# A two-layer attention trunk on one core: the softmax maximum is written already negated and scaled, and the step that scaled it goes

## The chip, the cores and the metric

The kernel runs on one core of a Trainium2 chip. The metric is device time in microseconds (us) of one execution, from three runs of each kernel. The engines are named as in the profile: PE (TensorE, with PEld for its weight loads), DVE (VectorE), ACT (ScalarE), POOL (GpSimd) and SP (SyncE, which here issues the DMAs). Each engine works through a fixed list of instructions in order and waits on semaphores that the other engines raise.

## What is computed

Two equal layers over 1024 tokens of width 1024. Each layer has two attention branches and a channel mixer; only the attentions' softmaxes matter here.

```python
# neighbourhood attention, 8 heads of 64: scores over an 8x16 window, scale = 64 ** -0.5 = 0.125
s = jnp.einsum('bhcd,ibhcjd->bhcij', q_r, k_nb).astype(jnp.float32) * scale
s = s + bias.transpose(0, 2, 1, 3)[None].astype(jnp.float32)
p = jax.nn.softmax(s.reshape(B, H, GRID_W, kh * kw), axis=-1)
...
# latent attention, 8 heads: q = rmsnorm(c_q, g_q) @ w_uq, scale = 96 ** -0.5
s = (jnp.einsum('bhqd,bkhd->bhqk', qn_b, k_nope)
     + jnp.einsum('bhqr,bkr->bhqk', qr_b, k_r))
p = jax.nn.softmax(s.astype(jnp.float32) * scale, axis=-1).astype(v.dtype)
```

`g_q` is a gain of 256 values per layer that multiplies the normalised latent before `w_uq` makes both parts of the query from it.

## The kernel before

One layer runs in stages, each of which keeps PE as the engine that all others feed: a token projection, the neighbourhood attention (NA) with the gate projections as filler between its units, the latent attention (MLA), a merge of both branches, an output projection, and the channel mixer. Everything is float32; products that need full precision are done as three matmuls of split operands (`mm3`, lines 208 to 210), so that a matmul of 512 columns is by far the commonest PE instruction.

**NA** (lines 595 to 641): 64 units a layer, each 128 queries by 384 keys. `unit_a` multiplies into the PSUM tile `sna` (L601), adds the bias table and takes the row maximum in one DVE instruction (L605), scales that maximum by -0.125 in a second, one column wide (L607), takes the exponential on ACT with the scaled maximum as its bias (L608), the reciprocal of the row sum on DVE (L609), and normalises on POOL (L610). `unit_b` transposes the result on PE (L618) and copies it to SBUF, half of the units on DVE (L621) and half on ACT (L623); `unit_c` multiplies by the values (L632).

**MLA** (lines 790 to 840): 64 units a layer, each 128 queries by 1024 keys. `unit_a` makes the scores in `smla`, a PSUM tile of two banks of which two are in rotation (six matmuls, L796), takes the maximum (L798), scales it by -96^-0.5 (L799), takes the exponential (L801), the reciprocal (L802), and normalises on POOL (L803). `unit_b` transposes (eight matmuls, L815) and copies the one half on ACT (L821), the other on DVE (L819); `unit_c` multiplies by the values (L830), 16 matmul instructions for every four units, which the trace records as 32. I call four units with their `unit_c` a block; there are 16 blocks a layer. Between the units stand the steps that prepare the next pair of heads (`prep_q` and `prep_k`, tiles `pqn` and `pkn`, with casts on ACT at L530 and subtractions on DVE at L531), and towards the end the loads and splits of the NA output for the merge (L852).

The order of an engine's list is not the order in which the code is written. The program is recorded unit by unit, and then a scheduler with its own estimate of every instruction's duration places each instruction on its engine where its inputs would be ready by that estimate. So a change of one DVE instruction can move matmuls. The exponential of unit n must have ended before the scores of unit n+2 are written, since two `smla` tiles rotate, and POOL must have normalised unit n before its transposes. These two are waits of PE.

Of the kernel before, what the change touches and what calls it, by code (L numbers as in the profile page):

```python
# [12 lines left out]
AF = mybir.ActivationFunctionType  # L13
ALU = mybir.AluOpType
AX = mybir.AxisListType
# [10 lines left out]
MLA_SCALE = 96 ** -0.5  # L26
# [11 lines left out]
def hybrid_trunk(  # L38
# [6 lines left out]
    V, A, G, T = nc.vector, nc.scalar, nc.gpsimd, nc.tensor  # L45
    depth = w_in.shape[0]
# [43 lines left out]
    def bank(s="pb"):  # L90
        return psb.tile([P, CH], F32, tag="pb", name=nm(s))
# [16 lines left out]
    col0 = {}  # L108
    cols = const.tile([P, 256], F32, name="cols")
# [11 lines left out]
    def turn_rows(t, n, base):  # L121
        ps = bank("pcols")
        tc.keep_in_program_order(T.transpose(ps[:, :n], t[:n, :], ident[:n, :n]))
        V.tensor_copy(cols[:, base:base + n], ps[:, :n])
# [55 lines left out]
    def ada_turn(l, j, acc):  # L180
        m = mods[l]
        for hh in range(2):
            ps = bank("pada")
            for k in range(4):
                T.transpose(ps[:, k * P:(k + 1) * P], acc[:, (4 * hh + k) * P:(4 * hh + k + 1) * P], ident)
            s = slice(8 * j + 4 * hh, 8 * j + 4 * hh + 4)
            V.tensor_reduce(m[:, s], ps[:].rearrange("p (a b) -> p a b", b=P), axis=AX.X, op=ALU.add)
        b0 = col0["b_ada"] + 48 * l + 8 * j
        V.tensor_tensor(m[:, 8 * j:8 * j + 8], m[:, 8 * j:8 * j + 8], cols[:, b0:b0 + 8], op=ALU.add)
        if j in (1, 4):  # L190
            t, g = (amix[l], "g_mix") if j == 1 else (amlp[l], "g_mlp")
            g0 = col0[g] + 8 * l
            V.tensor_scalar(t, m[:, 8 * j:8 * j + 8], 1.0, None, op0=ALU.add)
            V.tensor_tensor(t, t, cols[:, g0:g0 + 8], op=ALU.mult)
# [96 lines left out]
    ps = bank("ppos")  # L291
# [51 lines left out]
    for ch in range(2):  # L343
        for k in range(8):
            ps = bank("pyT")
# [10 lines left out]
    turn_rows(ta, na_, 0)  # L356
    turn_rows(tb, nb_, 128)

    ada_turn(0, 1, acc1)
    last = ada_sum(acc0, first_shift[5:], 5, pin)  # L360
    xT = [slab("xT") for _ in range(8)]
# [179 lines left out]
    def na_steps(l, h):  # L541

        tabs = {}
        for hd in range(2):
            for rg in range(2):
                t = pool["na"].tile([P, 12, 96], F32, name=nm(f"tab{hd}{rg}"))
                G.memset(t, NEG)
                tabs[hd, rg] = t

        def tables(pair, hd, rg):  # L550
            for r in range(8):
                row = 8 * rg + r
                st = min(max(row - 4, 0), 8)
                d0 = st - row + 7
                k0 = st - 4 * rg
                nc.sync.dma_start(tabs[hd, rg][r * 16:(r + 1) * 16, k0:k0 + 8, :], u_d[2 * pair + hd, :, d0:d0 + 8, :])

        st, vts = {}, {}

        def qk_weights(pair, n):  # L560
            st["w"] = whalves(kblock(w_in[l], (4 * n + pair) * P))

        def qk_unit(pair, n, ch):
            if ch == 0:
                st[pair, n] = [slab("st", dt=F32R) for _ in range(2)]
            ps = dense(st["w"], h[ch])
            for hd in range(2):
                dst = st[pair, n][hd][:, cs(ch)]
                if n == 0:
                    view = lambda t: t.rearrange("p (g r c) -> p r g c", g=4, c=16)  # L570
                    stacks(dst, ps[:].rearrange("p (r g c) -> p r g c", g=4, c=16), hd, view)
                else:
                    stacks(dst, ps, hd)

        def k_swap(pair):
            st[pair, 2] = [slab("st", dt=F32R) for _ in range(2)]
            for hd in range(2):
                swapped(st[pair, 2][hd], st[pair, 1][hd])

        def values(pair):  # L580
            vt = []
            for wi, w in enumerate(NA_WIN):
                if wi % 2 == 0:
                    vs = slab("vna", (P, 2, 4, P))
                for blk in range(4):
                    nc.sync.dma_start(
                        vs[:, wi % 2, blk, :],
                        v_d[:].rearrange("(b r c) d -> b r c d", r=4, c=64)[blk, :, w:w + 32, pair * P:(pair + 1) * P],
                    )
                vt.append(vs[:, wi % 2])  # L590
            vts[pair] = vt

        pts, po = {}, {}

        def unit_a(pair, rg, cg, hd):
            q1, k1, k2 = (st[pair, n][hd] for n in range(3))
            w = NA_WIN[cg]
            ps = pool["na_ps"].tile([P, 12, 32], F32, tag="S", name=nm("sna"))
            qs = q1[:, rg * CH + cg * P:rg * CH + (cg + 1) * P]
            for i, kk in enumerate((k1, k2)):  # L600
                T.matmul(ps, qs, kk[:].rearrange("p (r c) -> p r c", c=64)[:, 4 * rg:4 * rg + 12, w:w + 32],  # L601
                         start=i == 0, stop=i == 1)
            pt = pool["na"].tile([P, 12, 32], F32, tag="P", name=nm("pna"), bufs=4)
            sm = small()
            V.tensor_tensor_reduce(pt, ps, tabs[hd, rg][:, :, NA_KIND[cg] * 32:(NA_KIND[cg] + 1) * 32],  # L605
                                   op0=ALU.add, op1=ALU.max, scale=1.0, scalar=-3e38, accum_out=sm[:, 0:1])
            V.tensor_scalar(sm[:, 1:2], sm[:, 0:1], -0.125, None, op0=ALU.mult)  # L607
            A.activation(pt, pt, AF.Exp, bias=sm[:, 1:2], scale=0.125, accum_out=sm[:, 2:3])  # L608
            V.reciprocal(sm[:, 3:4], sm[:, 2:3])  # L609
            G.tensor_scalar(pt, pt, sm[:, 3:4], 1.0, op0=ALU.mult, op1=ALU.mult)  # L610
            pts[pair, rg, cg, hd] = pt

        def unit_b(pair, rg, cg, hd):
            pt = pts[pair, rg, cg, hd]
            pT = bank("pTna")
            pf = pt[:].rearrange("p a b -> p (a b)")
            for j in range(3):
                T.transpose(pT[:, j * P:(j + 1) * P], pf[:, j * P:(j + 1) * P], ident)  # L618
            t = pool["na"].tile([P, 384], F32, tag="pT", name=nm("ptna"), bufs=7)
            if (cg + hd) % 2:  # L620
                V.tensor_copy(t, pT[:, :384])  # L621
            else:
                A.copy(t, pT[:, :384])  # L623
            pts[pair, rg, cg, hd] = t

        def unit_c(pair, rg, cg):
            if cg == 0:
                po[pair, rg] = pool["na_ps"].tile([P, CH], F32, tag="po", name=nm("pona"))
            p = po[pair, rg]
            for j in range(3):  # L630
                for hd in range(2):
                    T.matmul(p[64 * hd:64 * hd + 64, cg * P:(cg + 1) * P],  # L632
                             vts[pair][cg][:, j + rg, 64 * hd:64 * hd + 64],
                             pts[pair, rg, cg, hd][:, j * P:(j + 1) * P], start=j == 0, stop=j == 2)
            if cg == 3:
                o = tmp("ona")
                V.tensor_copy(
                    o[:].rearrange("p (r g c) -> p r g c", g=4, c=16),
                    p[:].rearrange("p (g r c) -> p r g c", g=4, c=16),
                )  # L640
                nc.sync.dma_start(o_d[pair * P:(pair + 1) * P, cs(rg)], o)

        return qk_weights, qk_unit, k_swap, values, tables, unit_a, unit_b, unit_c


    def mla_steps(l):
# [143 lines left out]
        def unit_a(pair, q2, hd, qi):  # L790
            q1, k1, k2, qr = st[pair, hd]
            t = slice(q2 * 256 + qi * P, q2 * 256 + (qi + 1) * P)
            ps = pool["S"].tile([P, 1024], F32, tag="S", name=nm("smla"))
            for ch in range(2):
                for i, (a, b) in enumerate(((q1, k1), (q1, k2), (qr, d["Kr"]))):
                    T.matmul(ps[:, cs(ch)], a[:, t], b[:, cs(ch)], start=i == 0, stop=i == 2)  # L796
            sm = small()
            V.reduce_max(sm[:, 0:1], ps, axis=AX.X)  # L798
            V.tensor_scalar(sm[:, 1:2], sm[:, 0:1], -MLA_SCALE, None, op0=ALU.mult)  # L799
            pt = pool["mla"].tile([P, 1024], F32, tag="P", name=nm("pmla"), bufs=5)  # L800
            A.activation(pt, ps, AF.Exp, bias=sm[:, 1:2], scale=MLA_SCALE, accum_out=sm[:, 2:3])  # L801
            V.reciprocal(sm[:, 3:4], sm[:, 2:3])  # L802
            G.tensor_scalar(pt, pt, sm[:, 3:4], 1.0, op0=ALU.mult, op1=ALU.mult)  # L803
            pts[pair, q2, hd, qi] = pt
# [741 lines left out]
```

## Time and profile before

| | us |
|---|---|
| median of three runs | 3155.43 (3143.63 to 3157.5) |
| the profiled execution | 3154.83 |
| its span, first to last instruction | 3153.0 |
| PE busy in it | 3033.6 (96%) |
| DVE busy | 2069.4 (66%) |
| ACT busy | 1471.2 (47%) |
| POOL busy | 373.0 (12%) |

The profiled execution lies 0.6 us under the median, and 1.8 us of its time lie outside its span. A matmul's end in this profile is modelled and overlaps the next matmul's start, so a busy PE can hide short waits; where that matters, the starts of matmuls are compared. A row of the view by line gives the busy time, the mean duration in ns, and then the idle time of that engine just before such instructions with what ended it. NA runs from about 187 to 520 us and from 1735 to 2067 us, MLA from 520 to 765 us and from 2067 to 2311 us.

### The profile page before, as it was taken

Reading aid. Unit: us, or ns where it says so; the run is one execution under the profiler, and the core shown is the slowest. Engines: PE = TensorE matmul, PEld = TensorE weight load, DVE = VectorE, ACT = ScalarE, POOL = GpSimd, SP = SyncE. Lnnn points to the kernel's source line nnn. Section 1 sums busy time; section 2 is a strip of 40 time slices with the busy share of each in tenths; the row PEclk is TensorE's granted clock in tenths of the full one; section 3 lists DMA queues with packets and bytes.
Section 4 is the critical chain, followed back from the end, with each engine's and each line's share of the span. In section 5 each row is a group of like instructions: output and inputs, shape, how many; then the busy total and the mean of one; then the engine's idle time right before and its main releaser. Section 6 shows DMA issues by size and latency. Waiting matters only on the chain. (4 is left out here: it accounts for less than half of the span.)

```text
span 3153.0 us, 43333 instructions
## 1 busy us (share of the span) xinstructions
PE 3033.6 (96%) x15104; PEld 2456.0 (78%) x15104; DVE 2069.4 (66%) x3911; ACT 1471.2 (47%) x2820; POOL 373.0 (12%) x518
## 2 busy tenths in 40 slices
PE   7999999999998999999989999999999999999998
PEld 6878886776786888888777788777777778888887
DVE  8534436767859776877774334466775697767775
ACT  6234446554127666433352444555522466663332
POOL 5111002232200000000011011123221000000000
PEclk9999999999999999999999999999999999999999
DMA  6554334214853656856334444431266255586652
GB/s 258 157 135 111 99 109 119 63 36 145 280 191 107 244 207 231 293 196 209 106 121 138 125 121 114 117 86 36 73 214 218 69 180 214 211 308 205 215 166 84
DMA packets 359540, 497.56 MB, mean 158 GB/s; under 512 B 30556, under 2 KB 238618, under 8 KB 359322
## 3 DMA queue, kind: packets, MB, share of 16 engines
q1 hardware_dynamic: 359322, 494.80, 48.9%
q8 instruction: 119, 1.95, 0.3%
q14 instruction: 99, 0.81, 0.1%
HBM read 335.41 MB, written 141.98 MB: 151 GB/s over the span
## 5 line engine op out<-in xcount | busy, mean ns | idle before, releaser
L208 PE MATMUL pd<-h,wh 128*128 128x512 f32 x768 | 307.0, 400 | 0.6 <-ACT wh L201 0.6
L210 PE MATMUL pd<-h,wh 128*128 128x512 f32 x768 | 300.7, 392 | 0.0
L209 PE MATMUL pd<-h,wh 128*128 128x512 f32 x768 | 300.1, 391 | 0.0
L208 PE MATMUL pxz<-ho,wq 128*128 128x512 f32 x672 | 259.9, 392 | 3.5 <-DVE xT L1401 3.0
L209 PE MATMUL pxz<-ho,wq 128*128 128x512 f32 x672 | 261.8, 390 | 0.5 <-DVE ho L1153 0.5
L210 PE MATMUL pxz<-ho,wq 128*128 128x512 f32 x672 | 257.0, 389 | 0.0
L201 ACT CAST wq<-s 128x512 fp32r<-128x512 f32 (+3 forms) x296 | 154.5, 541 | 125.5 <-PE pxz L210 54.2
L208 PE MATMUL px<-h,wq 128*128 128x512 f32 x512 | 202.2, 396 | 3.5 <-ACT u L1242 2.3
L1401 DVE SCALAR_TENSOR_TENSOR xT<-pxz,mod,xT 128x512 f32<-128x512 f32 x252 | 186.7, 744 | 28.4 <-PE pxz L210 28.3
L798 DVE TENSOR_REDUCE sm<-smla 128x1 f32<-128x1024 f32 x128 | 156.6, 1223 | 69.7 <-PE smla L796 63.3
L209 PE MATMUL px<-h,wq 128*128 128x512 f32 x512 | 200.2, 392 | 1.4 <-DVE h L202 1.4
L210 PE MATMUL px<-h,wq 128*128 128x512 f32 x512 | 199.6, 391 | 0.0
L801 ACT ACTIVATE pmla<-smla,sm 128x1024 f32<-128x1024 f32 x128 | 143.0, 1117 | 118.2 <-DVE sm L799 113.3
L803 POOL TENSOR_SCALAR pmla<-pmla,sm 128x1024 f32<-128x1024 f32 x128 | 144.6, 1130 | 330.4 <-DVE sm L799 153.7
L202 DVE TENSOR_TENSOR wq<-s,wq 128x512 fp32r<-128x512 f32 (+3 forms) x296 | 168.7, 582 | 6.9 <-ACT wq L201 6.9
L796 PE MATMUL smla<-st,st 128*128 128x512 f32 x512 | 170.4, 413 | 2.9 <-ACT pmla L801 2.9
L208 PEld LDWEIGHTS pd<-h,wh 128*128 128x128 f32 x768 | 144.9, 189 | 32.4 <-issue 3.4
L210 PEld LDWEIGHTS pd<-h,wh 128*128 128x128 f32 x768 | 144.6, 188 | 32.8 <-issue 1.0
L209 PEld LDWEIGHTS pd<-h,wh 128*128 128x128 f32 x768 | 145.1, 189 | 28.3
L201 ACT CAST wq<-wr 128x384 fp32r<-128x384 f32 (+3 forms) x218 | 114.7, 539 | 106.2 <-PE pxz L210 62.6
L209 PE MATMUL pyz<-h,wq 128*128 128x512 f32 x384 | 151.6, 395 | 8.0 <-DVE h L202 8.0
L208 PEld LDWEIGHTS pxz<-ho,wq 128*128 128x128 f32 x672 | 126.1, 188 | 36.3 <-issue 4.8
(281 smaller groups left out, 7344.3 us busy)
## 6 DMA issues: line engine op xcount, KB each, us to landing
hid_d<-diff SPq DMA_DIRECT2D x112, 512.0 KB
ho<-hid_d SPq DMA_DIRECT2D x112, 512.0 KB
wada<-in_w_ada_dram SPq DMA_DIRECT2D x96, 512.0 KB
wr<-in_w_ff_dram SPq DMA_DIRECT2D x64, 512.0 KB
w<-in_w_in_dram SPq DMA_DIRECT2D x56, 512.0 KB
wr<-in_w_ff_dram SPq DMA_DIRECT2D x64, 384.0 KB
ho<-hid_d SPq DMA_DIRECT2D x84, 256.0 KB
hid_d<-u SPq DMA_DIRECT2D x68, 256.0 KB
```

Source lines behind the costliest of these rows:

```text
L201: pin(A.copy(dst_hi, src))
L202: V.tensor_tensor(dst_lo, src, dst_hi.bitcast(F32), op=ALU.subtract)
L208: T.matmul(ps, wh, mh, start=first and i == 0, stop=False, **kw)
L209: T.matmul(ps, wh, ml, start=False, stop=False, **kw)
L210: T.matmul(ps, wl, mh, start=False, stop=i == n - 1, **kw)
L796: T.matmul(ps[:, cs(ch)], a[:, t], b[:, cs(ch)], start=i == 0, stop=i == 2)
L798: V.reduce_max(sm[:, 0:1], ps, axis=AX.X)
L801: A.activation(pt, ps, AF.Exp, bias=sm[:, 1:2], scale=MLA_SCALE, accum_out=sm[:, 2:3])
L803: G.tensor_scalar(pt, pt, sm[:, 3:4], 1.0, op0=ALU.mult, op1=ALU.mult)
L1401: V.scalar_tensor_tensor(x, ps, gate_m[:, nt:nt + 1], x, op0=ALU.mult, op1=ALU.add)
```

## The change

In both softmaxes the instruction that takes the maximum now writes the exponential's bias itself. In NA the sum of scores and table is multiplied by -0.125 in the same instruction and the minimum is taken, so that the tile holds the negated, scaled scores and the minimum is the bias; the exponential then reads the tile with a scale of -1. In MLA the reduction writes its result with the sign turned; the factor 96^-0.5 goes into `g_q`, which is scaled once, right after the gains are loaded (four columns, one DVE instruction at line 360 of the changed kernel), and so into every query. The exponential then has no scale. The two one-column instructions at L607 and L799, 128 each, are gone. After the change the lines of NA's softmax are 608, 610, 611 and 612, and those of MLA's 798, 800, 802, 803 and 804.

```diff
     turn_rows(tb, nb_, 128)
 
+    gq = cols[:, col0["g_q"]:col0["g_q"] + 2 * depth]
+    V.tensor_scalar(gq, gq, MLA_SCALE, None, op0=ALU.mult)
+
     ada_turn(0, 1, acc1)
...
             V.tensor_tensor_reduce(pt, ps, tabs[hd, rg][:, :, NA_KIND[cg] * 32:(NA_KIND[cg] + 1) * 32],
-                                   op0=ALU.add, op1=ALU.max, scale=1.0, scalar=-3e38, accum_out=sm[:, 0:1])
-            V.tensor_scalar(sm[:, 1:2], sm[:, 0:1], -0.125, None, op0=ALU.mult)
-            A.activation(pt, pt, AF.Exp, bias=sm[:, 1:2], scale=0.125, accum_out=sm[:, 2:3])
+                                   op0=ALU.add, op1=ALU.min, scale=-0.125, scalar=3e38, accum_out=sm[:, 0:1])
+            A.activation(pt, pt, AF.Exp, bias=sm[:, 0:1], scale=-1.0, accum_out=sm[:, 2:3])
...
             sm = small()
-            V.reduce_max(sm[:, 0:1], ps, axis=AX.X)
-            V.tensor_scalar(sm[:, 1:2], sm[:, 0:1], -MLA_SCALE, None, op0=ALU.mult)
+            V.reduce_max(sm[:, 0:1], ps, axis=AX.X, negate=True)
             pt = pool["mla"].tile([P, 1024], F32, tag="P", name=nm("pmla"), bufs=5)
-            A.activation(pt, ps, AF.Exp, bias=sm[:, 1:2], scale=MLA_SCALE, accum_out=sm[:, 2:3])
+            A.activation(pt, ps, AF.Exp, bias=sm[:, 0:1], accum_out=sm[:, 2:3])
```

Every engine has the same instructions as before except for these on DVE, but the scheduler places many of them elsewhere, all of them between the start of NA and the end of MLA in each layer; the channel mixer's lists are unchanged. Two places show it, both in the sixth block of the first layer's MLA. The first is PE's list there: `smla` are the scores, `pTm` the transposes, `pom` the product with the values; the numbers differ between the two programs because each counts its own tiles. Before:

```order
L796 MATMUL smla_5640<-Kr_4500,st_5112 128x512
L815 MATMUL pTm_5697<-ident,pmla_5597 128x128 x4
L815 MATMUL pTm_5703<-ident,pmla_5597 128x128 x4
L830 MATMUL pom_5709<-PT_5528,vmla_4422 64x256
L796 MATMUL smla_5683<-st_5102,st_5101 128x512
L796 MATMUL smla_5683<-st_5103,st_5101 128x512
L796 MATMUL smla_5683<-Kr_4500,st_5104 128x512
L796 MATMUL smla_5683<-st_5102,st_5101 128x512
L796 MATMUL smla_5683<-st_5103,st_5101 128x512
L796 MATMUL smla_5683<-Kr_4500,st_5104 128x512
L830 MATMUL pom_5709<-PT_5601,vmla_4422 64x256
```

and the same place now:

```order
L798 MATMUL smla_5554<-Kr_4450,st_5041 128x512
L798 MATMUL smla_5596<-st_5031,st_5030 128x512
L798 MATMUL smla_5596<-st_5032,st_5030 128x512
L798 MATMUL smla_5596<-Kr_4450,st_5033 128x512
L798 MATMUL smla_5596<-st_5031,st_5030 128x512
L798 MATMUL smla_5596<-st_5032,st_5030 128x512
L798 MATMUL smla_5596<-Kr_4450,st_5033 128x512
L816 MATMUL pTm_5609<-ident,pmla_5512 128x128 x4
L816 MATMUL pTm_5615<-ident,pmla_5512 128x128 x4
L831 MATMUL pom_5621<-PT_5445,vmla_4374 64x256
L831 MATMUL pom_5621<-PT_5516,vmla_4374 64x256
```

The scores of the next unit moved ahead of the transposes of an earlier one, and the product with the values is no longer cut after its first matmul. Eight of the 16 blocks of a layer had the cut after one matmul; now none has.

The second place is DVE's list around the same units (`sm` are the one-column results, `PT` the copies of the transposes). Before:

```order
L798 TENSOR_REDUCE sm_5594<-smla_5587 128x1
L819 COPY PT_5601<-pTm_5608 128x4x128
L799 TENSOR_SCALAR sm_5594<-sm_5594 128x1
L798 TENSOR_REDUCE sm_5621<-smla_5614 128x1
L819 COPY PT_5601<-pTm_5634 128x4x128
L802 RECIPROCAL sm_5594<-sm_5594 128x1
L799 TENSOR_SCALAR sm_5621<-sm_5621 128x1
L819 COPY PT_5654<-pTm_5661 128x4x128
L798 TENSOR_REDUCE sm_5647<-smla_5640 128x1
```

and now:

```order
L800 TENSOR_REDUCE sm_5510<-smla_5503 128x1
L820 COPY PT_5516<-pTm_5523 128x4x128
L800 TENSOR_REDUCE sm_5536<-smla_5529 128x1
L803 RECIPROCAL sm_5510<-sm_5510 128x1
L820 COPY PT_5516<-pTm_5548 128x4x128
L820 COPY PT_5567<-pTm_5574 128x4x128
L803 RECIPROCAL sm_5536<-sm_5536 128x1
L800 TENSOR_REDUCE sm_5561<-smla_5554 128x1
L800 TENSOR_REDUCE sm_5603<-smla_5596 128x1
```

Before, a copy stood between the maximum and its scaling; now nothing stands between the maximum and the exponential that reads it, and the reciprocal has moved ahead of the copy beside it.

## Rows read from the trace of the kernel before

**Rows 1.** The page's first part: busy us, share and instructions of each engine.
```profile
PE 3033.6 (96%) x15104; PEld 2456.0 (78%) x15104; DVE 2069.4 (66%) x3911; ACT 1471.2 (47%) x2820; POOL 373.0 (12%) x518
```

**Rows 2.** Busy us (and count) of PE, PEld, DVE, ACT, POOL; clock, DMA: MLA, mixer.
```profile
520.00:765.00 245.00, 236.43 (x1490) 175.48 (x1487) 166.96 (x313) 133.12 (x234) 72.28 (x64) 1.00 0.19 54
...
1200.00:1400.00 200.00, 199.55 (x877) 164.04 (x876) 149.93 (x269) 95.03 (x188) 0.00 (x0) 1.00 0.73 252
```

**Rows 3.** The view by line: count, busy us, mean ns, idle before and its releasers.
```profile
L799 DVE TENSOR_SCALAR sm<-sm 128x1 f32<-128x1 f32 x128 | 18.5, 144 | 1.0
L607 DVE TENSOR_SCALAR sm<-sm 128x1 f32<-128x1 f32 x128 | 18.1, 148 | 0.8
...
L798 DVE TENSOR_REDUCE sm<-smla 128x1 f32<-128x1024 f32 x128 | 156.6, 1223 | 69.7 <-PE smla L796 63.3 <-PE pTm L815 5.2
...
L605 DVE CUSTOM_DVE_ANT_1 pna<-sna,tab 128x384 f32<-128x384 f32 x128 | 69.2, 551 | 69.4 <-PE sna L601 68.4 <-PE pTna L618 0.8
```

**Rows 4.** The same view: the transposes of MLA and of NA.
```profile
L815 PE MATMUL pTm<-ident,pmla 128*128 128x128 f32 x1024 | 130.8, 274 | 14.0 <-POOL pmla L803 13.6
...
L618 PE MATMUL pTna<-ident,pna 128*128 128x128 f32 x384 | 65.3, 282 | 7.2 <-POOL pna L610 6.9
```

**Rows 5.** Who waited for whom: us in total, times, longest.
```profile
ACT pmla L801 <- DVE sm L799: 113.3, 92, 4.7
...
PEld pTm L815 <- POOL pmla L803: 28.9, 36, 2.1
```

**Rows 6.** PE in order of time in that block: start, length, idle before.
```profile
595.35 1.91 PE L815 MATMUL pTm<-ident,pmla 128*128 128x128 f32 x16
597.01 0.70 PE L796 MATMUL smla<-st,st 128*128 128x512 f32 x2
...
598.24 0.40 PE L796 MATMUL smla<-Kr,st 128*128 128x512 f32 x1
598.85 1.09 PE L815 MATMUL pTm<-ident,pmla 128*128 128x128 f32 x8 [0.22 <-POOL pmla L803]
599.88 0.65 PE L830 MATMUL pom<-PT,vmla 128*64 128x256 f32 x2
600.45 0.73 PE L796 MATMUL smla<-st,st 128*128 128x512 f32 x2
```

**Rows 7.** DVE in order of time, the same block.
```profile
593.36 1.23 DVE L798 TENSOR_REDUCE sm<-smla 128x1 f32<-128x1024 f32 x1 [1.23 <-PE smla L796]
594.50 0.68 DVE L819 COPY PT<-pTm 128x512 f32<-128x512 f32 x1
595.10 0.14 DVE L799 TENSOR_SCALAR sm<-sm 128x1 f32<-128x1 f32 x1
...
596.75 0.68 DVE L819 COPY PT<-pTm 128x512 f32<-128x512 f32 x1
597.35 0.15 DVE L802 RECIPROCAL sm<-sm 128x1 f32<-128x1 f32 x1
```

**Rows 8.** ACT and POOL in the same block.
```profile
595.33 1.12 ACT L801 ACTIVATE pmla<-smla,sm 128x1024 f32<-128x1024 f32 x1 [0.97 <-DVE sm L799]
...
597.67 1.13 POOL L803 TENSOR_SCALAR pmla<-pmla,sm 128x1024 f32<-128x1024 f32 x1 [5.35 <-DVE sm L799]
```

**Rows 9.** Stretches of one block each, columns as in rows 2.
```profile
591.59:605.63 14.04, 13.82 (x89) 10.12 (x88) 8.41 (x17) 6.96 (x12) 4.49 (x5) 1.00 0.03 11
607.13:622.72 15.59, 15.59 (x102) 12.13 (x100) 13.59 (x23) 10.24 (x19) 3.38 (x3) 1.00 0.31 74
```

**Rows 10.** PE in order of time: the start of MLA and its last blocks.
```profile
524.84 0.73 PE L796 MATMUL smla<-st,st 128*128 128x512 f32 x2 [1.44 <-ACT pmla L801]
...
730.94 1.09 PE L815 MATMUL pTm<-ident,pmla 128*128 128x128 f32 x8 [1.27 <-POOL pmla L803]
```

**Rows 11.** PE in order of time: the end of the first NA.
```profile
514.88 0.55 PE L618 MATMUL pTna<-ident,pna 128*128 128x128 f32 x3 [1.71 <-POOL pna L610]
```

**Rows 12.** Who waited for whom, SP's DMA queue: the longest wait of a table load.
```profile
SPq L556 <- DVE sm L605: 22.6, 8, 4.6
```

## The prediction

> **What bounds the kernel.** I read the page's first part, then the waits, then one block of units in order of time. PE is busy for 3033.6 of the span's 3153.0 us and DVE for 66% of it [rows 1], so DVE's time as such buys nothing: a change on DVE is worth only what PE waits for it. [...] The two instructions to be removed last 144 and 148 ns, 128 of each, 36.6 us of DVE in all, and DVE hardly idles before them [rows 3]. Nobody on PE waits for them directly. But the exponential on ACT waited 92 times for L799, 113.3 us in all, and the transposes' weight loads waited 36 times for POOL, which comes after the exponential, 28.9 us in all [rows 5]; PE's own idle time there is 13.6 us in MLA and 6.9 us in NA [rows 4]. So the chain from maximum to transposes ends last at certain places of PE's list, and it runs through the removed instruction.
>
> How it runs is seen in one block. The maximum starts at 593.36 and ends at 594.59. Then comes a copy, because the scheduler placed it there, and the scaling starts only at 595.10 [rows 7]; the exponential starts at 595.33 [rows 8], 0.09 after the scaling's end. Without the scaling it could start 0.09 after the maximum, at 594.68: 0.65 us earlier, of which the instruction itself is only 0.14. Its reciprocal then waits behind the next maximum and another copy until 597.35 [rows 7], POOL works from 597.67 to 598.80 [rows 8], and the transposes start at 598.85 [rows 6], when the scores before them are done: the last of these started at 598.24, and a matmul of 512 columns takes 200 / 877 = 0.228 us from start to start [rows 2], so PE was free at 598.47 and lost 0.38 us. The row shows 0.22 of it as idle, since a matmul's end is modelled 0.16 later.
>
> **What a block costs with and without the waits.** The block from 591.59 has 88 weight loads in 14.04 us. The block from 607.13 has the same units' work and 12 matmuls of the preparation, 100 loads in 15.59 us, with PE busy throughout [rows 9]. Less 12 x 0.228 = 2.74 it is 12.85 us. So the first kind of block loses 1.19 us: 0.38 at the transposes, and the rest at the cut of `pom` (two matmuls at 599.88, then scores only at 600.45 [rows 6]) and in short gaps.
>
> **The change part by part.** *Blocks with the cut.* There are eight a layer, and the new order, shown with the change, puts the scores of one more unit before the transposes and leaves `pom` whole. One unit's scores take 598.47 - 597.01 = 1.46 us [rows 6], so the transposes would stand at 599.93, 1.13 us after POOL was done even in the old trace. The wait at the transposes goes, and so does the cut. At most that is 16 x 1.19 = 19.0 us. Late next are the scores that moved up: they need the exponential of two units before. From the end of that unit's scores PE now has 16 transposes (597.01 - 595.35 = 1.66 [rows 6]) and one unit's scores (1.46), 3.12 us; maximum and exponential need, with 0.09 for each handover, 0.09 + 1.23 + 0.09 + 1.12 = 2.53 [rows 7, 8]. A margin of 0.59. I take three quarters, 14 us, for gaps that stay; half, 9.5, is the lower end.
>
> *The other waits for POOL in MLA.* All 36 waits cost 13.6 us of shown idle plus 36 x 0.16 of modelled ends, 19.4 us; 16 x 0.38 = 6.1 of it is counted above, so 13.3 us are left in 20 waits at the beginning and end of MLA, the long one of 1.27 us among them [rows 10]. Their chain gets shorter by 0.14 us at least and by 0.65 where a copy stood between: from 20 x 0.14 = 2.8 to 13.3. With waits of 0.67 on average against 0.65, but some much longer, I take half, 6.5 us.
>
> *NA.* Its transposes waited 6.9 us for POOL [rows 4], 1.71 of it in the last units of the first layer [rows 11]; elsewhere gate projections fill PE. The scheduler puts a few transposes earlier, before part of a `pona` product, which takes back what the shorter chain gives. From nothing to 6.9; I take 2 us, the end alone. The first wait of MLA, 1.44 us for an exponential whose maximum had nothing behind it [rows 10], shrinks by 0.14: nothing.
>
> *The new forms.* The trace has neither a reduction that turns its sign nor the minimum form of L605. The nearest rows are the old forms, 1223 and 551 ns [rows 3]. Less is excluded, since each element is still read once; if the sign cost as much as the instruction it replaces, they would last 1367 and 699 ns, and only the copy's place would be gained. I take no difference, since constants and operators change and the shapes do not, and keep the other end for the range. [...] The exponential without its scale keeps its form: 1.12 us.
>
> *The scaling of `g_q`.* One instruction of about 0.14 us before the first layer, beside loads: 0 to 0.15, I take nothing.
>
> *SP's queue.* DMAs change places by little in NA and MLA; the one that moves furthest is one of eight loads of a bias table, which now stands ahead of two swaps of keys. A table load waited 4.6 us at most [rows 12], but another load of the same table, with the same wait, already stood ahead of them: nothing, 4.6 us at worst.
>
> *The rest of DVE's 36.6 us* lies beside PE's work: nothing. If that cover were gone it would show in MLA, where DVE is busy 167 of 245 us [rows 2]; it has 78 us to spare.
>
> **Sum:** 14 + 6.5 + 2 = 22.5 us, from 9.5 + 2.8 = 12 to about 34 (19.0, with 10 of the 13.3 and 5 of the 6.9). The profiled execution took 3154.8, close to the median of 3155.4, so the forecast is **3133 us**, its own range 3121 to 3142. A measurement of this kernel can tell about 0.5%, 15.8 us, from no change.
>
> **Rivals.**
> *Only the latency counts.* The new order makes as many gaps as it closes, and only shorter chains remain: 36 x 0.14 to 0.2, 5 to 7 us, so 3149. For it: the scheduler goes by estimates, and old ones put copies before the scaling. Against it: the margins of 1.13 and 0.59 us.
>
> *Nothing changes.* PE is the bound, 96% busy, and the waits are filled by others. 3155. The rows of waits speak against it, as each ends just after POOL does. [...]
>
> *Slower: scores wait for a buffer.* The moved scores find the tile still read by the exponential of two units before. That decides where the maximum starts more than 0.59 us after that handover; with two copies ahead (1.36 us) each moved unit waits 0.77. If two units of each of the 32 blocks do, PE loses 64 x 0.77 = 49 us and gains 22: 3182. It is slower by more than 0.5% from 0.6 us each. For it: such a wait exists, 1.44 us at the start of MLA [rows 10]. Against it: the new list has one copy ahead of the deciding maximum, of transposes that end 1.46 us before its scores do.
>
> *The new forms are slow.* If the reduction took twice its time, DVE would have 167 + 64 x 1.08 = 236 of 245 us in MLA, and the chain would be 1.2 us longer where it now is 0.65 shorter: about +20, 3175. Nothing in the trace speaks for it.
>
> **How the numbers follow.** Forecast 0.64, latency only 0.13, nothing 0.13, buffer wait 0.07, slow forms 0.03. A small part of the forecast's own range lies within 15.8 us, 0.04. So faster by over 0.5%: 0.60; within: 0.04 + 0.13 + 0.13 = 0.30; slower: 0.10. The range 3121 to 3154 takes in the forecast, the latency case and half of the nothing case; left out are 0.10 of slower, 0.06 of nothing and some 0.03 below.
>
> **What would show it.** Right: no row for the two scalings; 1223 and 551 ns as before; the weight loads' wait for POOL down from 28.9 to 10 us or less; the block without preparation at about 13 us; MLA at about 235 us a layer instead of 245, and NA within 2 us of its 333. Wrong: scores that wait for the exponential by more than 10 us in all (buffers), a longer reduction (forms), or blocks still of 14 us with gaps elsewhere (order).

## The result, and the profile after

The changed kernel takes 3117.81 us, median of five runs (3112.85 to 3118.17), against 3155.43; the ratio is 0.988 with a 95% interval of 0.9867 to 0.9893. That is faster by 37.6 us where 22.5 were forecast, and it lies 3 us below the low end of the range. The profiled execution took 3118.17 us, its span 3116.4.

By the starts of the first score matmul of a stage and of its last `pom`, MLA went from 244.4 and 244.1 us to 228.9 and 228.9 (30.7 us in all), NA, up to MLA's first score matmul, from 333.4 and 331.9 to 329.4 and 330.4 (5.5 us). All other stages together came out within 1 us of what they were.

The page's first part of the changed kernel, against [rows 1]:

```profile
PE 3006.2 (96%) x15104; PEld 2455.0 (79%) x15104; DVE 2050.7 (66%) x3656; ACT 1465.4 (47%) x2820; POOL 369.2 (12%) x518
```

DVE has 256 instructions less and one more, for `g_q`. It lost 18.7 us of busy time and not 36.6, since a scaling began while the copy ahead of it still ran (595.10, and 594.50 + 0.68 in [rows 7]). PE lost 27.4 us with the same number of matmuls. The two stretches of MLA now, columns as in [rows 2]:

```profile
517.40:746.40 229.00, 225.22 (x1487) 175.58 (x1486) 162.02 (x249) 132.63 (x234) 71.96 (x64) 1.00 0.20 58
...
2045.20:2274.20 229.00, 225.25 (x1487) 175.57 (x1486) 162.03 (x249) 132.59 (x234) 72.02 (x64) 1.00 0.20 58
```

PE's granted clock is 1.00 in both, as in MLA before [rows 2], so the clock explains nothing here. The view by line, against [rows 3, 4]:

```profile
L800 DVE TENSOR_REDUCE sm<-smla 128x1 f32<-128x1024 f32 x128 | 156.4, 1222 | 42.3 <-PE smla L798 36.6 <-POOL pmla L804 2.6
...
L816 PE MATMUL pTm<-ident,pmla 128*128 128x128 f32 x1024 | 132.1, 273 | 5.2 <-POOL pmla L804 5.2
L831 PE MATMUL pom<-PT,vmla 128*64 128x256 f32 x1024 | 120.1, 383 | 0.0
...
L608 DVE CUSTOM_DVE_ANT_1 pna<-sna,tab 128x384 f32<-128x384 f32 x128 | 69.6, 552 | 74.6 <-PE sna L604 68.0 <-PE pTna L620 5.8 <-issue 0.4
L634 PE MATMUL pona<-ptna,vna 128*64 128x128 f32 x768 | 69.0, 287 | 0.8 <-ACT ptna L625 0.5
L620 PE MATMUL pTna<-ident,pna 128*128 128x128 f32 x384 | 64.4, 278 | 4.5 <-POOL pna L612 3.8 <-ACT vmla L738 0.5
```

The two reductions last what they did, 1222 and 552 ns: sign, factor and minimum cost nothing. PE's idle time before MLA's transposes fell from 14.0 to 5.2 us. The row to keep in mind is `pom`. It shows no idle time in either kernel, so no wait, and yet its busy time fell too. This is the row of the kernel before:

```profile
L830 PE MATMUL pom<-PT,vmla 128*64 128x256 f32 x1024 | 131.6, 384 | 0.0
```

The view of waits, against [rows 5]:

```profile
ACT pmla L802 <- DVE sm L800: 47.8, 48, 3.8
...
PEld pTm L816 <- POOL pmla L804: 6.9, 4, 2.0
...
PEld smla L798 <- ACT pmla L802: 4.1, 5, 1.6
```

The exponential waits 48 times for DVE instead of 92, the transposes 4 times for POOL instead of 36, and the scores that moved up hardly wait for an exponential.

PE in order of time shows what is behind the `pom` row. In the kernel before, where it is cut after its first matmul [rows 6] and goes on after the next scores (columns: start, length, then line, operation and count of records; 32 records are the 16 matmuls):

```profile
601.71 0.40 PE L796 MATMUL smla<-Kr,st 128*128 128x512 f32 x1
602.04 3.67 PE L830 MATMUL pom<-PT,vmla 128*64 128x256 f32 x30
605.64 0.50 PE L208 MATMUL pqn<-cqh,uqn 128*128 128x512 f32 x1
```

And whole, in the changed kernel:

```profile
592.16 3.67 PE L831 MATMUL pom<-PT,vmla 128*64 128x256 f32 x32
595.77 0.50 PE L208 MATMUL pqn<-cqh,uqn 128*128 128x512 f32 x1
```

All sixteen take 595.77 - 592.16 = 3.61 us from their start to the next work. The fifteen that are left after the cut take 605.64 - 602.04 = 3.60. So the one before the cut, 600.45 - 599.88 = 0.57 us [rows 6], is nearly all extra. ([Rows 6] show it as two records; it is one matmul, and not two, as the prediction says.) With the step from scores to `pom`, 602.04 - 601.71 = 0.33 us where the next scores would have followed after 0.23, this cut costs 0.57 - 0.01 + 0.10 = 0.66 us of PE, and no row shows it as a wait. The kernel before has 54 runs of `pom` for its 32 products, so 22 cuts (most often the eight a layer after one matmul; all stand after an odd number of matmuls); the changed one has 36 runs, 4 cuts.

### The profile page after: what moved, and what is told of

Same layout as the page of the kernel before. It is cut to its first block, busy times and chain, and to the rows that moved or that the text cites. A ratio compares the mean times of both kernels' runs of the same rounds, so it can differ in the third digit from the quotient of the medians.

```text
span 3116.4 us, 43063 instructions
## 1 busy us (share of the span) xinstructions
PE 3006.2 (96%) x15104; PEld 2455.0 (79%) x15104; DVE 2050.7 (66%) x3656; ACT 1465.4 (47%) x2820; POOL 369.2 (12%) x518
## 5 line engine op out<-in xcount | busy, mean ns | idle before, releaser
L800 DVE TENSOR_REDUCE sm<-smla 128x1 f32<-128x1024 f32 x128 | 156.4, 1222 | 42.3 <-PE smla L798 36.6
L523 DVE TENSOR_SCALAR gate<-pd,cols 128x512 f32<-128x512 f32 x64 | 48.0, 751 | 161.3 <-PE pd L210 155.7
```

Of the source, the lines that this page charges most:

```text
L800: V.reduce_max(sm[:, 0:1], ps, axis=AX.X, negate=True)
```

## The experiments

The theory to be tested: MLA's gain has two parts, the shorter chain, which closes waits for POOL, and the new order of PE's list. The rivals: it is DVE's freed time that counts, or only one of the two, or NA. Totals are compared with the kernel before on the same chip; stages are compared in the profiles, since the unchanged stretch between the two layers' attentions alone varies from 964.1 to 975.6 us among these runs; in its last third PE's granted clock was 0.98 in the kernel before, in the changed one and in MLA's part alone, and 0.97 in the run of 975.6 us, the version with the products cut less. A profile is one execution, and the stages of before are those of its one profile. The results together:

| kernel | median us | ratio to before (95%) | NA, two layers | MLA, two layers |
|---|---|---|---|---|
| before | 3155.43 | | 333.4, 331.9 | 244.4, 244.1 |
| changed | 3117.81 | 0.988 (0.9867 to 0.9893) | 329.4, 330.4 | 228.9, 228.9 |
| MLA's part alone | 3124.28 | 0.991 (0.9895 to 0.9924) | 332.8, 333.8 | 229.5, 228.9 |
| NA's part alone | 3145.4 | 0.9976 (0.9966 to 0.9985) | 329.5, 328.7 | 243.9, 244.2 |
| changed, old order in MLA | 3134.36 | 0.9945 (0.9931 to 0.996) | 329.6, 328.6 | 238.4, 238.2 |
| before, new order in MLA | 3141.47 | 0.9966 (0.9953 to 0.9979) | 333.3, 331.8 | 238.3, 236.9 |
| changed, DVE's time put back | 3114.69 | 0.9875 (0.986 to 0.989) | 330.9, 327.6 | 229.6, 229.8 |
| before, scaling on ACT | 3137.72 | 0.9951 (0.9936 to 0.9965) | 332.2, 330.9 | 239.0, 239.3 |
| before, `pom` whole | 3141.64 | 0.9961 (0.9949 to 0.9973) | 333.3, 331.3 | 237.5, 237.1 |
| changed, old order, `pom` whole | 3114.1 | 0.988 (0.9865 to 0.9894) | 329.1, 328.6 | 229.1, 228.9 |
| before, scaled twice, old order | 3177.49 | 1.0078 (1.0063 to 1.0093) | 333.3, 331.2 | 256.2, 258.7 |
| changed, products cut less | 3105.5 | 0.9844 (0.9828 to 0.9861) | 326.5, 323.3 | 227.2, 227.3 |
| the same, reciprocal on ACT | 3116.84 | 0.9878 (0.9859 to 0.9898) | 328.3, 326.7 | 230.1, 231.2 |

**Each half alone.** The edits are the parts of the change's diff: NA's hunk alone, and MLA's with the scaling of `g_q`.

> MLA's part of the change alone, with the scaling of g_q; NA's softmax as in the kernel before. PE's list in MLA is then the changed kernel's but for a few units at its start. Theory (the gain is MLA's waits): MLA 229 to 230 us a layer as in the changed kernel (244 before), NA as before at 333 and 332, in all -28 to -32 us against the kernel before, ratio 0.990 to 0.991. Rival 1 (the DVE time taken out counts wherever it is, half of it here): about -19 us, ratio 0.994. Rival 2 (the gain comes from NA): under -10 us.

> NA's part of the change alone; MLA's softmax and g_q as in the kernel before. Theory: NA's two stages 2 to 6 us shorter together, MLA 244 us a layer as before, in all -2 to -6 us, ratio 0.998 to 0.9995. Rival 1 (DVE time taken out counts wherever it is): about -19 us, ratio 0.994. Rival 2 (the gain comes from NA): -30 us, ratio 0.990.

MLA's part gives 28 us, NA's part 7 (stages: 3.9 and 3.2). NA gave somewhat more than I had written down; the rest is as the theory had it. So four fifths of the gain are MLA's, and there is no 19 us in each half for DVE's time.

**Chain and order apart.** Each kernel was given the other's order of PE in MLA, by edges that bind only the order on PE; the other engines' lists are the scheduler's own. In the list S are the scores of a unit, T its two groups of transposes, O a `pom`; a star gives the number of matmuls.

```diff
+PE_ORDER = (
+    "S0 S1 S2 T0a T0b S3 T1a T1b S4 T2a T2b S5 ... O2*1 S16 O2*15 S17 ..."
...
+        def pin_order():
+            last = None
+            for word in PE_ORDER[l].split():
+                tag, _, n = word.partition("*")
+                for _ in range(int(n) if n else len(listed[tag])):
+                    ins = listed[tag].pop(0)
+                    if last is not None:
+                        tc.add_manual_dep(ins, last.name, ...)
+                    last = ins
```

> The changed kernel with PE's list in MLA pinned to the order of the kernel before (cuts of pom and transposes ahead of the next scores); no scaling on the chain. Theory A (the shorter chain alone closes the waits, in whatever order): MLA 229 to 232 us a layer, in all within 6 us of the changed kernel, ratio 0.988 to 0.990. Theory B (the gain is the new order): MLA 241 to 244, in all -4 to -12 us against the kernel before, ratio 0.996 to 0.999. My own guess, both: MLA 234 to 239, ratio about 0.993.

> The kernel before with PE's list in MLA pinned to the changed kernel's order; the scaling stays on the chain and in DVE's list, in both softmaxes. Theory A (the shorter chain): MLA stays at 241 to 246 us a layer, because the scores that moved up now wait for exponentials that come 0.65 us later than in the changed kernel; ratio 0.998 to 1.002. Theory B (the order): MLA 229 to 232, ratio 0.989 to 0.991. My own guess, both: MLA 233 to 239, ratio about 0.994.

Neither theory alone: the chain gives 6.0 and 5.9 us at the old order, the order 6.1 and 7.2 at the old chain, and both together 15.5 and 15.2. By line, the old order with the short chain (`pom`, and the transposes with their weight loads):

```profile
L880 PE MATMUL pom<-PT,vmla 128*64 128x256 f32 x1024 | 131.6, 384 | 3.3 <-ACT PT L870 3.3
L864 PE MATMUL pTm<-ident,pmla 128*128 128x128 f32 x1024 | 129.5, 273 | 5.0 <-POOL pmla L851 4.8
L864 PEld LDWEIGHTS pTm<-ident,pmla 128*128 128x128 f32 x1024 | 117.1, 141 | 22.4 <-POOL pmla L851 9.9 <-issue 0.8
```

Most of the waits for POOL are gone without any change of order, 28.9 to 9.9 us, and `pom` costs its old 131.6. The new order with the long chain, scores, transposes and `pom`:

```profile
L843 PE MATMUL smla<-st,st 128*128 128x512 f32 x512 | 174.7, 419 | 8.3 <-ACT pmla L848 8.2
L863 PE MATMUL pTm<-ident,pmla 128*128 128x128 f32 x1024 | 133.0, 273 | 7.2 <-POOL pmla L850 7.0
L879 PE MATMUL pom<-PT,vmla 128*64 128x256 f32 x1024 | 120.1, 383 | 0.0
```

In the kernel before, the first of these rows was:

```profile
L796 PE MATMUL smla<-st,st 128*128 128x512 f32 x512 | 170.4, 413 | 2.9 <-ACT pmla L801 2.9
```

At the new order `pom` has its new 120.1, and the scores wait for exponentials, 8.2 us instead of 2.9: the rival of the late buffer is real with the long chain, only small: 5.3 us more, where the whole order gains 13.3.

**What in the order counts.** The kernel before, its own order, and each cut `pom` whole where its last part stood; then the same order with the short chain.

```diff
-    ... O2*1 S16 O2*15 S17 ...
+    ... S16 O2 S17 ...
```

> The kernel before with PE's list in MLA pinned to its own order, except that each product with the values that was cut stands whole, where its last part stood; the chain and DVE's list keep the scaling. 54 runs of pom become 32. Theory (a cut has a fixed price on PE of some 0.65 us: the starts of the 16 runs cut after one matmul add up to that, with no wait in them): 22 cuts less at 0.5 to 0.65 us are -11 to -14 us in two layers, MLA 237 to 239 us a layer, ratio 0.9955 to 0.9965. Rival (the time at a cut is a wait for something later, and appears elsewhere): MLA 243 to 245, ratio 0.999 to 1.001.

> The changed kernel with PE's list in MLA pinned to the order of the kernel before, but each pom whole where its last part stood: the short chain and no cuts, and still transposes ahead of the next unit's scores. Theory (two terms that add: the shorter chain was worth 6.0 us a layer at the old order, the cuts 6.9 at the old chain): 244.3 - 6.0 - 6.9 = 231.4, MLA 230 to 233 us a layer, ratio 0.989 to 0.991; what is left to the changed kernel's 228.9 is the place of the scores. Rival (the moved scores matter more, and without them the waits at the transposes come back when pom no longer covers them): MLA 234 to 238, ratio 0.992 to 0.9945.

Whole products alone give 6.9 and 7.0 us a layer, 13.9 / 22 = 0.63 us a cut, as the starts had said. And with the short chain the old order without cuts is as fast as the changed kernel, 229.1 and 228.9, although the transposes stand ahead of the next scores again. The rival that I gave it was wrong, and so was my additive figure of 231.4. Its rows (transposes, their loads and `pom`):

```profile
L862 PE MATMUL pTm<-ident,pmla 128*128 128x128 f32 x1024 | 129.2, 273 | 4.1 <-POOL pmla L849 4.0
L878 PE MATMUL pom<-PT,vmla 128*64 128x256 f32 x1024 | 117.6, 382 | 3.2 <-ACT PT L868 3.2
L862 PEld LDWEIGHTS pTm<-ident,pmla 128*128 128x128 f32 x1024 | 117.4, 141 | 20.5 <-POOL pmla L849 7.9
```

So most of the order's worth is that `pom` is not cut. The place of the scores is worth something too, though the stage's total hides it. These are the twelve middle blocks of the first layer, from the first scores of the sixth unit to those of the 54th, in this kernel and in the changed one (columns as in [rows 2]):

```profile
529.05:697.13 168.08, 166.07 (x1105) 129.23 (x1103) 115.99 (x183) 99.41 (x171) 55.58 (x50) 1.00 0.18 47
...
527.67:693.74 166.07, 166.07 (x1111) 130.67 (x1109) 117.45 (x182) 98.18 (x172) 55.47 (x51) 1.00 0.18 48
```

PE is busy for 166.07 us in both, and only with the old order does it idle, for 2.0 us a layer. The changed kernel gives about as much back outside these blocks, where its 4 cuts are (4 x 0.63 = 2.5 us in two layers). That the two parts give 4.7 us more together than apart (30.5 against 11.9 + 13.9) fits the rows of the kernel before with whole `pom`: PE, no longer held by the cuts, waits longer for the old chain, 8.6 us at the scores where it had waited 2.9. No run tests that reading.

```profile
L841 PE MATMUL smla<-st,st 128*128 128x512 f32 x512 | 170.9, 414 | 8.6 <-ACT pmla L846 8.6
```

**DVE's time, or its place in the queue.** First the changed kernel with a scaling that nobody reads; then the kernel before with its scaling on ACT. MLA's edit is shown; NA has the same.

```diff
             V.reduce_max(sm[:, 0:1], ps, axis=AX.X, negate=True)
             ...
             A.activation(pt, ps, AF.Exp, bias=sm[:, 0:1], accum_out=sm[:, 2:3])
+            V.tensor_scalar(sm[:, 1:2], sm[:, 0:1], -MLA_SCALE, None, op0=ALU.mult)
```

```diff
-            V.tensor_scalar(sm[:, 1:2], sm[:, 0:1], -MLA_SCALE, None, op0=ALU.mult)
+            A.mul(sm[:, 1:2], sm[:, 0:1], -MLA_SCALE)
```

> The changed kernel, with the one-column scaling put back into DVE's list in both softmaxes as an instruction that nobody reads: DVE has its old number of instructions and its old time, the chain stays short, and PE's list is the changed kernel's but for some 20 rows. Theory (the chain and the order count, DVE's time does not): as the changed kernel within 5 us, ratio to the kernel before 0.988 to 0.990, MLA 229 to 230 us a layer. Rival (the gain is DVE's 36.6 us): the gain goes, ratio 0.998 to 1.0, MLA 240 to 244.

> The kernel before, with the scaling of the maximum done by ACT, just ahead of its exponential, in both softmaxes: DVE has its time back and no copy can stand between maximum and scaling, but the step stays on the chain, at about 0.2 us (the nearest one-column rows of ACT are 193 ns) and one more handover of 0.09. PE's list keeps eight cuts of pom a layer, in the middle and no longer after one matmul. Theory (queue place and cuts): the waits for POOL shrink as in the old-order run and the cuts cost less than 0.65 us each, MLA 234 to 239 us a layer, ratio 0.992 to 0.996. Rival 1 (DVE's time is what counts): as the changed kernel, ratio 0.988 to 0.990. Rival 2 (any step on the chain costs the same wherever it is done): ratio 0.998 to 1.001.

With its old instructions back on DVE the changed kernel keeps its gain, 0.9875. The rows of the two idle scalings:

```profile
L804 DVE TENSOR_SCALAR sm<-sm 128x1 f32<-128x1 f32 x128 | 18.7, 146 | 1.6
L611 DVE TENSOR_SCALAR sm<-sm 128x1 f32<-128x1 f32 x128 | 18.1, 146 | 0.9
```

They take 36.8 us of DVE, where those in [rows 3] took 36.6, and cost nothing that the total shows. On ACT the step stays on the chain at 204 ns, PE's list keeps 20 cuts of `pom` (52 runs) where I had expected 16, and the gain is less than half of the whole, 0.9951 against 0.988; in MLA it is a third, 10.2 of 30.7 us. Here 6 of the 20 cuts fall between two pairs of matmuls.

```profile
L799 ACT ACTIVATE sm<-sm 128x1 f32<-128x1 f32 x128 | 26.1, 204 | 87.7 <-DVE sm L798 87.4
```

Matched one by one in the traces, the time from the end of MLA's maximum to the start of its exponential is 0.92 us on average before, 0.50 with the scaling on ACT, and 0.19 after the change. An instruction of 144 ns had cost 0.73. The way from the exponential's end to POOL's start moved too, for the reciprocal between them stands in DVE's queue as well: 1.11 us before, 1.00 after the change, 0.81 in the changed kernel with the old order.

**The same cost, doubled.** A multiplication by one between scaling and exponential in MLA; PE's order pinned to that of the kernel before.

```diff
             V.tensor_scalar(sm[:, 1:2], sm[:, 0:1], -MLA_SCALE, None, op0=ALU.mult)
+            V.tensor_scalar(sm[:, 0:1], sm[:, 1:2], 1.0, None, op0=ALU.mult)
```

> The kernel before with a second one-column step on the chain of MLA's softmax (a multiplication by one between the scaling and the exponential), PE's list in MLA pinned to the order of the kernel before, so that only the chain changes. Theory (a step on the chain costs its place in DVE's queue, 0.14 to 0.8 us an exponential, and PE feels it where the chain ends last): +3 to +8 us a layer, MLA 247 to 252, ratio 1.002 to 1.005. Rival 1 (only the instruction's own 0.14 us counts): MLA 245 to 246.5, ratio 1.0005 to 1.0015. Rival 2 (hidden): no change.

It costs 11.8 and 14.6 us a layer, twice what taking the first step out had given at the same order, and more than any of my figures. Maximum to exponential is now 1.42 us, 0.50 more; exponential to POOL is 0.90, 0.21 less, so POOL comes only 0.29 later. PE's idle time before the transposes hardly grew, from 14.0 to 15.1 us, and the new wait is at the scores:

```profile
L843 PE MATMUL smla<-st,st 128*128 128x512 f32 x512 | 175.2, 422 | 18.9 <-ACT pmla L849 18.9
```

With one step the scores had hardly waited for an exponential, 2.9 us; the second is felt there.

**Versions to beat both.** The products with the values start with the tile that comes last, so that the scheduler cuts them less; then the same with the reciprocal made on ACT.

```diff
-            for kk in range(4 * half, 4 * half + 4):
-                for hd in range(2):
+            for kk in range(4 - 4 * half, 8 - 4 * half):
+                for hd in (1, 0):
...
-                na_c(pair, rg, cg - 1)
                 na_c(pair, rg, cg)
+                na_c(pair, rg, cg - 1)
```

```diff
-            V.reciprocal(sm[:, 3:4], sm[:, 2:3])
+            A.activation(sm[:, 3:4], sm[:, 2:3], AF.Ln)
+            A.activation(sm[:, 3:4], sm[:, 3:4], AF.Exp, scale=-1.0)
```

> The changed kernel, with the products with the values in both attentions written so that the tile that comes last is used first (second head before first, later keys or later unit first), which lets the scheduler keep them whole: runs of pona go from 76 to 38, runs of pom stay 36 with four broken pairs less. Theory (a cut has a price on PE; for pona, whose pairs take half the time, 0.2 to 0.3 us): -8 to -12 us against the changed kernel, ratio to the kernel before 0.984 to 0.986, NA 325 to 327 us a layer. Rival (cuts in NA are hidden, or the later products hold buffers): as the changed kernel or slower, ratio 0.988 to 0.992.

> The version with whole products, and the reciprocal of both softmaxes taken off DVE too: ACT makes it as the exponential of minus the logarithm, right behind its own exponential. It takes out DVE's queue between the row sum and POOL (0.63 us on average in MLA) and puts in two one-column instructions of ACT, about 0.2 us each by the nearest rows (193 ns), so the chain is some 0.2 to 0.4 us shorter on average. Theory: at most the waits for POOL that are left (3.1 and 3.3 us of PE's idle time there), -2 to -6 us against the version with whole products, ratio to the kernel before 0.9825 to 0.984. Rival (ACT becomes the queue: its copies and exponentials come later): the same or slower, 0.9845 to 0.988.

The first is the fastest version, 0.9844 (0.9828 to 0.9861), 9 us below the changed kernel with the idle scalings, which ran beside it. `pona`, in 38 runs instead of 76, shows it:

```profile
L634 PE MATMUL pona<-ptna,vna 128*64 128x128 f32 x768 | 52.5, 282 | 1.8 <-ACT ptna L625 1.8
```

against 69.0 in the changed kernel, though PE's idle time before NA's transposes rose from 4.5 to 9.6 us. In MLA `pom` keeps 36 runs, and the stage is 1.7 and 1.6 us shorter. The reciprocal on ACT loses the gain again. Its two instructions take 205 and 204 ns,

```profile
L804 ACT ACTIVATE sm<-sm 128x1 f32<-128x1 f32 x128 | 26.2, 205 | 2.6
L805 ACT ACTIVATE sm<-sm 128x1 f32<-128x1 f32 x128 | 26.0, 204 | 2.2
```

and they stand ahead of ACT's exponentials and copies; MLA is 2.9 and 3.9 us longer. That ACT's queue is the cause is argued from the rows and not shown; loading of activation tables is not, since there are three `ACT_TABLE_LOAD` here as in the changed kernel.

## Why the prediction was wrong, step by step

*What bounds the kernel*: right. PE is 96% busy in both kernels, and the change was worth what PE had waited, and more. The rival that nothing changes fell: DVE is at 66% before and after, and the edit gave 1.2%. The kernel with the idle scalings, at 0.9875, shows that DVE's busy time is worth nothing here; the place of one instruction on the way to PE is, 0.73 us from maximum to exponential.

*Blocks with the cut*: the step that failed, in its size. I took 16 blocks at 1.19 us, 19.0, and of that "three quarters, 14 us, for gaps that stay". Measured from the first scores of the sixth unit to those of the 54th, MLA's twelve middle blocks went from 178.4 to 166.1 us in the first layer and from 178.0 to 166.1 in the second, 24.2 us in all: more than the 19.0 that I had called the most. The first layer's before, to be set beside the changed kernel's line under "What in the order counts":

```profile
532.28:710.68 178.40, 175.15 (x1104) 130.28 (x1103) 120.57 (x232) 98.00 (x171) 55.53 (x50) 1.00 0.16 44
```

PE is now busy for the whole 166.07 us. Four of these blocks take 55.40 us, and without any wait they would take 4 x 12.85 + 18 x 0.228 = 55.5: no gap stayed. The error of 10.2 has two parts of about the same size. The quarter that I kept back, 5.0, was kept for waits, but 0.66 of the 1.19 us of such a block is no wait: it is the cut's own price on PE, and goes when the new list shows `pom` whole. That list stood with the change, and the 0.57 us in [rows 6]. And the 19.0 itself was 5.2 too low. I counted the 16 blocks that are cut after one matmul and priced them by the one that loses least. But four middle blocks took 14.04 + 15.54 + 15.58 + 14.40 = 59.56 us before, 4.1 more than without waits, where I had counted 19.0 / 6 = 3.2 for each of the six fours; three of the four lose, so 18 blocks do and not 16 (two are cut after eleven matmuls), and they lose 1.35 on average, not 1.19.

*The moved scores*: wrong as the reason for the transposes. I had let the transposes' wait go because one more unit's scores stand ahead of them. The short chain closes that wait at the old order too: without cuts, a block there takes 12.87 us, as good as the 12.85 without waits, although the scores have not moved. The margin of 0.59 us that I gave the moved scores held in the changed kernel. It counts 0.09 us from maximum to exponential; at the new order with the long chain this is 0.88 on average, so the margin is overdrawn by 0.2, and the scores wait those 8.2 us.

*The other waits for POOL*: 6.5 forecast. What is left of MLA's 30.7 us beside the middle blocks is 6.5, so the number was right. How much of it is waits for POOL stays open: PE's idle time before the transposes outside the middle blocks fell by 2.5 us, from 7.7 to 5.2, and the modelled ends hide the rest.

*NA*: 2 us forecast, 5.5 measured in the profile of the change, 7.1 with NA's part alone; the upper bound was 6.9. The step that failed is the taking back: I expected NA's products to be cut more and to give up what the shorter chain gains. PE's idle time before its transposes fell from 7.2 to 4.5 us, and `pona`, cut less often (76 runs for 86), from 70.9 to 69.0.

*New forms, `g_q`, SP*: nothing, as forecast. The reduction that turns its sign lasts 1222 ns against 1223, and the minimum form in NA 552 against 551.

*Of what would show it*, these held: forms, the wait for POOL under 10 us, the block near 13 us (12.82 in the changed kernel), scores waiting for exponentials well under 10. MLA at 235 and NA within 2 us of 333 did not.

## What to carry to other kernels

Where a scheduler fills the queues, price an instruction on a chain by its place in its engine's queue, not by its length (here 0.73 us against 144 ns): match producer and consumer in the trace and take the whole distance. When an edit lets a scheduler reorder, price what the new list shows as engine time (a run that is no longer cut, here 0.63 us a cut) apart from waits, and do not discount it as one. And where products come in pairs, try to write first the one that is ready last, so that less is put between them: in NA this halved the runs of `pona` (76 to 38), in MLA it left `pom` its 4 cuts.

## What the runs showed of the hardware

The two heads' products with the values, 64 columns each, run as pairs. The trace has two records for each matmul, so four for a pair. In a whole `pom` (the changed kernel's from 592.16) the records come two by two, the second 7 ns after the first, and the next two follow after 216 ns, only the second two after 267. A matmul without a partner takes as many of these steps as a pair: the two records of the last of the fifteen (the kernel before, from 602.04) start 216 ns apart. That is why fifteen matmuls took 3.60 us and sixteen 3.61. I had read the short `pom` as a gap.

The chain's price is not linear: taking 0.78 us off it (0.92 to 0.14, at the old order) gave 6.0 us a layer, and adding 0.50 took 13.2. The rows fit this: the first closed waits at the transposes (14.0 to 5.0 us of PE's idle time), and the second opened others at the scores (2.9 to 18.9). The distances are not the whole chain, whose end at POOL came 1.08 us earlier and 0.29 us later.
